# An fp32 first chunk, scores on row halves, and 512-column projections in a two-layer hybrid trunk

## The chip, the cores and the metric

The kernel runs on one core of a Trainium2 chip. The metric is the device time of one execution in microseconds (us). Before the change three runs took 942.56, 943.69 and 944.15 us, a median of 943.69 us. The profile below comes from one further execution.

TensorE (PE in the rows) multiplies matrices into PSUM; VectorE (DVE) and ScalarE (ACT) work on elements; GpSimd (POOL) does small masks and powers; SyncE (SP) issues nearly all DMAs.

## The reference

Two layers, each with a residual add, on 256 tokens of 1024 channels, all in float32:

```python
for layer in range(2):
    h = rmsnorm(x, norm_w)
    proj = h @ w_in          # 14368 columns: fq fk fv ff fg | sz sxbc sdt | dq dk dv dg | mg
    # A: softmax attention, 16 heads of 64, causal, scores shifted by cumulative log forget gates
    y_a = fox(fq, fk, fv, cumsum(log_sigmoid(ff))) * silu(fg)
    # B: causal depthwise conv (4 taps) + silu on x|B|C, chunked state-space scan, gated grouped norm
    y_b = rmsnorm_groups(ssd(silu(conv(sxbc)), softplus(sdt)) * silu(sz)) * ssm_norm_w
    # C: 8 heads of (softmax1 - lambda * softmax2) V, rotary on a quarter of q and k, per-head norm
    y_c = rmsnorm_heads(diff_attention(rope(dq), rope(dk), dv)) * silu(dg)
    gates = sigmoid(mg)      # three gates of 1024 channels
    merged = sum(gates[n] * (y[n] @ w_branch[n]) for n in (A, B, C))
    x = x + merged @ w_out
return rmsnorm(x, final_norm_w)
```

## The kernel before

**Projections.** All weights lie in HBM as *chunks* of at most 512 columns by 1024 rows, in the order in which they are used (`chunk_list`). A chunk is loaded in four *units* of 256 rows, 512 KB each, into a buffer `raw`. ScalarE rounds a unit to the one-pass format fp32r (`whi`, L231) and VectorE keeps what is left (`wlo`, L232). The activations are split the same way, and each product is the sum of three fp32r matmuls: hi by hi, hi by lo, lo by hi.

There are two forms. `bform` (L249) holds 128 tokens of the activation as the stationary operand and streams 512 weight columns: the result has tokens on partitions. `aform` (L264) holds 128 weight columns and streams all 256 tokens: the result has channels on partitions, as q, k, the conv inputs and the FoX gate need it. For one block of 128 columns and one of eight row blocks, `aform` issues three matmuls of 256 columns. One PSUM bank takes two column blocks, and the pool `pp` has three banks. There are 28 chunks in A form (14 in each layer) and 896 such triples.

**Around the projections.** `plan` lists the chunks of a layer as items. After each bank the loop calls `pump`, which lets waiting jobs (attention pairs, state-space groups, norms) emit a few instructions. A scheduler then orders each engine's instructions, so the order on an engine isn't that of the code.

**Scores.** q and k come out of `aform` with two heads on the two halves of the 128 partitions. `stack_q` and `stack_k` write, for each head, the hi and the lo part on top of each other (L380 to L388), so that two fp32r matmuls with 128 rows (L400, L401) give the head's scores. VectorE then adds the bias and takes the row maximum (L403), ScalarE takes the exponential (L406). For FoX the bias tile `sc` is loaded by two broadcast DMAs (L422, L423) from a scratch in HBM (`scr`, written at L371 from the cumulative gates that L359 to L366 compute), and GpSimd masks it twice (L426). There are 32 such head pairs in all, 16 in each layer: eight in FoX and eight in differential attention.

**The opening.** x is normalised, with the norm weight broadcast by DMA (L291, L210), transposed on TensorE (L198), split (L188, L189) and only then multiplied with the first chunk. TensorE transposes an identity 24 times first (L968).

**Buffers.** The pool `ap` has 41 pieces of 2 KB per partition; h's two halves take eight of them, the stacked q and k of four heads six. The PSUM pools `pp`, `pq`, `pt` have 3, 3 and 2 banks.

Of the kernel before, what the change touches and what calls it, by code (L numbers as in the profile page):

```python
# [34 lines left out]
WARM = 24  # L35
BEHIND = 1
ACTSQ = (2, 4)
# [12 lines left out]
def chunk_list():  # L50
    names = []
    names += [("fv0", [("w", FV, 512)]), ("fv1", [("w", FV + 512, 272)]),
              ("fv2", [("w", FV + 784, 240), ("w", FF, 16), ("w", SDT, 16)])]
# [6 lines left out]
             "mg10", "mg11", "wb10", "wb11", "mg20", "mg21", "wb20", "wb21", "wo0", "wo1"]  # L60
# [36 lines left out]
def trunk(ctx: ExitStack, tc: tile.TileContext, x, norm_w, weights, small, vectors,  # L97
# [13 lines left out]
    pq = ctx.enter_context(tc.tile_pool(name="pq", bufs=3, space=bass.MemoryType.PSUM))  # L111
    pt = ctx.enter_context(tc.tile_pool(name="pt", bufs=2, space=bass.MemoryType.PSUM))
# [9 lines left out]
    def halves():  # L122
        return tuple([a2(dtype=F32R) for _ in range(4)] for _ in range(2))

# [70 lines left out]
    def split_rows(src, hi, lo, tt, c):  # L195
        ps = bank(pt, "pt")
# [18 lines left out]
    def load_chunk(off, total, after=None, behind=()):  # L215
        units = []
        for u in range(UNITS):
            raw = wraw.tile([P, KU * 512], F32, name="raw")[:, 0:KU * total]
            o = off + u * KU * P * total
            ins = nc.sync.dma_start(raw, weights[o:o + KU * P * total].rearrange("(p f) -> p f", p=P)).ins  # L220
            if u == BEHIND:
                for late in behind:
                    tc.add_manual_dep(late, ins.name, mybir.DependencyInfo(
                        mybir.DependencyClass.NoSync, mybir.DependencyReason.DATA), reason="order")
            hi = wsp.tile([P, KU * 512], F32R, name="whi")[:, 0:KU * total]
            lo = wsp.tile([P, KU * 512], F32R, name="wlo")[:, 0:KU * total]
            with ExitStack() as es:
                if u > 0 and after:
                    for ins in after:
                        es.enter_context(tc.issue_after(ins))  # L230
                S.copy(out=hi, in_=raw)  # L231
                V.tensor_tensor(out=lo, in0=raw, in1=hi.bitcast(F32), op=ALU.subtract)  # L232
            units.append(tuple(t.rearrange("p (k n) -> p k n", k=KU) for t in (hi, lo)))
        return units, total

    ORDER = [(u, k, i) for u in range(UNITS) for k in range(KU) for i in range(3)]
    EARLY = [(u, k, i) for u, i in ((0, 0), (0, 1), (0, 2), (1, 0), (1, 2), (1, 1),
                                    (2, 0), (2, 2), (2, 1), (3, 0), (3, 2), (3, 1)) for k in range(KU)]
# [14 lines left out]
    def aform(ch, act, jj):  # L253
        units, n = ch
        ahi, alo = act
        ps = bank(pp, "pp")
        for u in range(UNITS):
            whi, wlo = units[u]
            for k in range(KU):
                kt = u * KU + k  # L260
                for j in range(2):
                    c0 = (2 * jj + j) * P
                    for i, (w, a) in enumerate(((whi, ahi), (whi, alo), (wlo, ahi))):
                        PE.matmul(ps[:, j * T:(j + 1) * T], lhsT=w[:, k, c0:c0 + P], rhs=at(a, kt),  # L264
                                  start=(kt == 0 and j == 0 and i == 0), stop=(kt == KT - 1 and j == 1 and i == 2))
        return ps

# [3 lines left out]
    def make_h(l, tt, xt, xs, ss, gap):  # L271
        st = L[l]
        if tt == 0:
            st["hT"] = halves()
# [54 lines left out]
    def small_chain(l, ps_by_tt):  # L329
# [26 lines left out]
        yield 2, 1.5  # L356
# [19 lines left out]
    LOH, HIH = slice(0, 64), slice(64, P)  # L376

    def stack_q(src, dst):
        for q, main, rest in zip(dst, (LOH, HIH), (HIH, LOH)):
            S.copy(out=q[main], in_=src[main])  # L380
            V.tensor_tensor(out=q[rest], in0=src[main], in1=q[main].bitcast(F32), op=ALU.subtract)

    def stack_k(src, dst):
        for k, kl, main, rest in zip(dst[0:2], dst[2:4], (LOH, HIH), (HIH, LOH)):
            S.copy(out=k[main], in_=src[main])
            V.tensor_tensor(out=kl[main], in0=src[main], in1=k[main].bitcast(F32), op=ALU.subtract)
            S.copy(out=k[rest], in_=src[main])
            S.copy(out=kl[rest], in_=kl[main].bitcast(F32))  # L388

    def split_qk(key, src):  # L390
        tiles = [a2(dtype=F32R) for _ in range(2 if key[1] == "q" else 4)]
        (stack_q if key[1] == "q" else stack_k)(src, tiles)
        return tiles

    def scores(st, pre, b, i, sc, bias, nm, rs):
        j, tk = b % 2, st[f"{pre}k{b // 2}"]
        q, k, kl = st[f"{pre}q{b // 2}"][i], tk[i], tk[2 + i]
        ps = bank(pq, "pq")
        for o, qs, n in ((0, slice(0, P), P), (P, slice(P, T), T)):
            PE.matmul(ps[:, o:o + n], lhsT=q[:, j, qs], rhs=k[:, j, 0:n], start=True, stop=False)  # L400
            PE.matmul(ps[:, o:o + n], lhsT=q[:, j, qs], rhs=kl[:, j, 0:n], start=False, stop=True)  # L401
        for t, sl in SPANS:
            V.tensor_tensor_reduce(out=sc[:, sl], in0=ps[:, sl], in1=bias[:, sl], scale=-0.125, scalar=BIG,  # L403
                                   op0=ALU.add, op1=ALU.min, accum_out=nm[:, t:t + 1])
        for t, sl in SPANS:
            S.activation(out=sc[:, sl], in_=sc[:, sl], func=AF.Exp, scale=-1.0,  # L406
                         bias=nm[:, t:t + 1], accum_out=rs[:, t:t + 1])
# [8 lines left out]
    def fox_pair(l, b, yhi, ylo):  # L416
# [7 lines left out]
        for i in (0, 2):  # L424
            v = sc[:, :, i * P:(i + 1) * P]
            G.affine_select(out=v, in_=v, pattern=[[0, 2], [-1, P]], compare_op=ALU.is_ge,  # L426
                            fill=NEG, base=0, channel_multiplier=1)
# [4 lines left out]
        for i in range(2):  # L432
            scores(st, "f", b, i, sc[:, i, :], sc[:, i, :], nm[:, i, :], rs[:, i, :])
# [58 lines left out]
    def ssd_cb(l):  # L492
# [16 lines left out]
        ps = bank(pt, "pt")  # L509
# [9 lines left out]
    def ssd_x(l, c, tt):  # L519
# [10 lines left out]
        ps = bank(pt, "pt")  # L530
# [12 lines left out]
    def ssd_group(l, g):  # L543
# [36 lines left out]
        ps = bank(pt, "pt")  # L580
# [67 lines left out]
    def rope(l, c):  # L648
# [19 lines left out]
        yield 1, 2.4  # L668
        for key, src in (("dq", q), ("dk", k)):
            for jj in range(2):  # L670
                st[f"{key}{2 * c + jj}"] = split_qk(key, src[jj])
            yield 1, 1.2 if key[1] == "k" else 2.4
# [6 lines left out]
    def diff_head(l, h):  # L679
        st, pr = L[l], par[l]  # L680
        yield from need(l, f"dq{h // 2}", f"dk{h // 2}")
        sc = sp.tile([P, 2, 384], F32, name="sc")
        nm = sm.tile([P, 2, 2], F32, name="dnm")
        rs = sm.tile([P, 2, 2], F32, name="drs")
        for i in range(2):
            scores(st, "d", h, i, sc[:, i, :], bmask, nm[:, i, :], rs[:, i, :])
# [40 lines left out]
    def plan(l):  # L727
# [39 lines left out]
        def t_evac(key):  # L767
            def f(jj, ps):
                st[f"{key[0:2]}{2 * int(key[2]) + jj}"] = split_qk(key, ps.rearrange("p (a t) -> p a t", t=T))
            return f  # L770

        def r_evac(key):
            def f(jj, ps):
                t = a2()
                st.setdefault("_" + key, []).append(t)
                S.copy(out=t, in_=ps.rearrange("p (a t) -> p a t", t=T))
                if jj == 1 and key[:2] == "dk":
                    start_job(rope, l, int(key[2]))
            return f

        def g_evac(key):
            def f(jj, ps):
                t = a2()
                p3 = ps.rearrange("p (a t) -> p a t", t=T)
                S.activation(out=t, in_=p3, func=AF.Tanh, scale=0.5)
                V.scalar_tensor_tensor(out=t, in0=t, scalar=1.0, in1=p3, op0=ALU.add, op1=ALU.mult)
                st[f"{key[0:2]}{2 * int(key[2]) + jj}"] = t
            return f

        def c_evac(key, j0):  # L790
# [11 lines left out]
            return f  # L802
# [90 lines left out]
        B("fv0", [v_evac("fv", 0, 512, False), v_evac("fv", 512, 272, False)])  # L893
        B("fv2", [v_evac("fv", 784, 240, True, fv_small)])
# [31 lines left out]
        mgroup(1)  # L926
        wgroup(1, "yB")
        mgroup(2)
# [12 lines left out]
        B("wb20", [wb_evac(2, 0), wb_evac(2, 1)], act=lambda: st["yC"], pre=load_res, wait="yC")  # L941
        B("wo0", [wo_evac(0), wo_evac(1)], act=lambda: st["mT"], flag="mT")
# [9 lines left out]
    def prefetch(n, after=None, behind=()):  # L952
        while queue and n > 0:
            l_, k_, _, off, m = queue.pop(0)
            loaded.append((l_, k_, load_chunk(off, m, after, behind)))
# [3 lines left out]
    xt = [rows() for _ in range(2)]  # L959

    def load_x(tt):
        for c in range(2):
            cs = slice(512 * c, 512 * c + 512)
# [101 lines left out]
```

## Time and profile before

| | |
|---|---|
| median of three runs | 943.69 us |
| profiled execution, its own time | 944.5 us |
| its span on the core | 942.8 us |
| PE busy | 928.9 us (99%) |
| DVE busy | 702.5 us (75%) |
| ACT busy | 596.7 us (63%) |
| DMA | 172.49 MB, mean 183 GB/s |

The profiled execution's own time is 1.7 us above its span. Busy time of PE counts a matmul to its modelled end, and consecutive matmuls overlap, so what a matmul costs is read from the distance between the starts of neighbours, not from its duration. A matmul of float32 operands that aren't fp32r shows as two records.

### The profile page before, as it was taken

Reading aid. Unit: us, or ns where it says so; the run is one execution under the profiler, and the core shown is the slowest. Engines: PE = TensorE matmul, PEld = TensorE weight load, DVE = VectorE, ACT = ScalarE, POOL = GpSimd, SP = SyncE. Lnnn points to the kernel's source line nnn. Section 1 sums busy time; section 2 is a strip of 40 time slices with the busy share of each in tenths; the row PEclk is TensorE's granted clock in tenths of the full one; section 3 lists DMA queues with packets and bytes.
Section 4 is the critical chain, followed back from the end, with each engine's and each line's share of the span. In section 5 each row is a group of like instructions: output and inputs, shape, how many; then the busy total and the mean of one; then the engine's idle time right before and its main releaser. Section 6 shows DMA issues by size and latency. Waiting matters only on the chain.

```text
span 942.8 us, 16557 instructions
## 1 busy us (share of the span) xinstructions
PE 928.9 (99%) x6076; PEld 831.4 (88%) x6076; DVE 702.5 (75%) x1440; ACT 596.7 (63%) x1131; POOL 37.2 (4%) x71
## 2 busy tenths in 40 slices
PE   6999999999999999999999999999999999999997
PEld 5999999988898988888889999998889999888886
DVE  5778788988666877864768778789877677787474
ACT  4668786655557868654546869666545596885441
POOL 1001100000000000100000110000000000010000
PEclk8999999999999999999999999999999999999999
DMA  7866735674555555555558664456646455554551
GB/s 223 278 208 205 218 112 158 188 242 148 176 188 177 181 185 171 167 163 197 190 176 279 195 222 137 140 179 201 203 155 197 158 186 190 190 171 155 181 184 45
DMA packets 60321, 172.49 MB, mean 183 GB/s; under 512 B 7312, under 2 KB 15824, under 8 KB 60240
## 3 DMA queue, kind: packets, MB, share of 16 engines
q1 hardware_dynamic: 59952, 170.91, 56.2%
q8 instruction: 48, 0.79, 0.3%
q10 hardware_dynamic: 288, 0.52, 0.1%
q14 instruction: 33, 0.27, 0.1%
HBM read 167.14 MB, written 2.16 MB: 180 GB/s over the span
## 4 chain that ended last, share of the span: by engine, by line
PE 90%; issue 7%; DMA 1%; DVE 0%; POOL 0%; ACT 0%; POOLq 0%; SPq 0%; DVEq 0%
PE pp L249 49%; PE pp L264 30%; PE pq L400 2%; PE pt L457 1%; PE pq L401 1%; PE pq L447 1%; PE pq L590 1%; PE pt L637 1%; PE pt L198 1%; PE pq L702 1%; PE pq L600 0%; PE pt L532 0%; DMA sc<-scr 0%; DMA scr<-sc_cum 0%; PE pt L709 0%
## 5 line engine op out<-in xcount | busy, mean ns | idle before, releaser
L249 PE MATMUL pp<-whi,a 128*128 128x512 f32 (+2 forms) x1488 | 451.3, 383 | 2.5 <-ACT a L188 1.6
L232 DVE TENSOR_TENSOR wlo<-raw,whi 128x1024 fp32r<-128x1024 f32 (+1 forms) x296 | 349.9, 1194 | 80.3 <-ACT whi L231 77.0
L231 ACT CAST whi<-raw 128x1024 fp32r<-128x1024 f32 (+1 forms) x296 | 302.1, 1028 | 119.3 <-PE pp L249 67.7
L264 PE MATMUL pp<-a,whi 128*128 128x256 f32 x1792 | 332.4, 285 | 0.0
L249 PEld LDWEIGHTS pp<-whi,a 128*128 128x128 f32 x1488 | 273.9, 188 | 55.8 <-ACT a L188 2.2
L264 PEld LDWEIGHTS pp<-a,whi 128*128 128x128 f32 x1792 | 281.2, 191 | 1.3 <-issue 1.0
L249 PE MATMUL pp<-wlo,a 128*128 128x512 f32 (+2 forms) x744 | 282.0, 381 | 0.1
L264 PE MATMUL pp<-a,wlo 128*128 128x256 f32 x896 | 254.4, 284 | 0.0
L264 PEld LDWEIGHTS pp<-a,wlo 128*128 128x128 f32 x896 | 171.5, 191 | 0.8 <-issue 0.8
L249 PEld LDWEIGHTS pp<-wlo,a 128*128 128x128 f32 x744 | 139.7, 188 | 25.8 <-DVE wlo L232 1.0
L477 DVE SCALAR_TENSOR_TENSOR a<-sw,pT,a 128x255 f32<-128x255 f32 (+2 forms) x96 | 42.0, 477 | 6.1 <-ACT a L474 6.0
L183 POOL TENSOR_TENSOR rstd<-rstd,mhalf 128x2 f32<-128x2 f32 (+2 forms) x24 | 17.8, 740 | 663.0 <-DVE rstd L181 642.1
L406 ACT ACTIVATE sc<-sc,dnm 128x128 f32<-128x128 f32 x64 | 28.6, 449 | 8.4 <-DVE dnm L403 8.3
L400 PE MATMUL pq<-a,a 128*128 128x128 f32 (+1 forms) x128 | 32.0, 285 | 0.5 <-DVE nm L403 0.5
L819 DVE SCALAR_TENSOR_TENSOR a<-a,pp 128x512 f32<-128x512 f32 x24 | 16.4, 683 | 20.6 <-PE pp L249 20.6
L188 ACT CAST a<-pt 128x256 fp32r<-128x256 f32 x32 | 11.4, 370 | 32.0 <-PE pt L198 25.8
L401 PE MATMUL pq<-a,a 128*128 128x128 f32 (+1 forms) x128 | 31.5, 269 | 0.0
L406 ACT ACTIVATE sc<-sc,nm 128x128 f32<-128x128 f32 (+1 forms) x64 | 28.4, 446 | 3.0 <-DVE nm L403 2.8
L403 DVE CUSTOM_DVE_ANT_0 sc<-pq,sc 128x128 f32<-128x128 f32 (+1 forms) x64 | 19.5, 351 | 7.4 <-POOL sc L426 6.6
L400 PEld LDWEIGHTS pq<-a,a 128*128 128x128 f32 x128 | 23.7, 190 | 1.3 <-DVE nm L403 0.9
L401 PEld LDWEIGHTS pq<-a,a 128*128 128x128 f32 x128 | 23.6, 191 | 0.3
L191 ACT ACTIVATE a<-pt,pT 128x256 fp32r<-128x256 f32 x32 | 14.8, 472 | 14.2 <-PE pt L637 12.4
(168 smaller groups left out, 811.8 us busy)
## 6 DMA issues: line engine op xcount, KB each, us to landing
raw<-in_weights_dram SPq DMA_DIRECT2D x280, 512.0 KB, 4.4
raw<-in_weights_dram SPq DMA_DIRECT2D x16, 272.0 KB, 3.4
sc<-scr SPq DMA_DIRECT2D x16, 256.0 KB, 5.6
a<-scr SPq DMA_DIRECT2D x16, 256.0 KB, 5.8
a<-in_x_dram SPq DMA_DIRECT2D x8, 256.0 KB, 5.4
sc<-scr SPq DMA_DIRECT2D x16, 128.0 KB, 5.2
a<-in_norm_w_dram SPq DMA_DIRECT2D x4, 256.0 KB, 7.0
rp<-a SPq DMA_DIRECT2D x32, 32.0 KB, 3.8
```

The source lines that it names most:

```text
L183: G.tensor_tensor(out=r[:, 0:width], in0=r[:, 0:width], in1=mhalf[:, 0:width], op=ALU.pow)
L191: S.activation(out=hi, in_=ps, func=AF.Copy, scale=scale)
L231: S.copy(out=hi, in_=raw)
L232: V.tensor_tensor(out=lo, in0=raw, in1=hi.bitcast(F32), op=ALU.subtract)
L249: PE.matmul(ps[:, 0:(c1 or n) - c0], lhsT=at(a, kt)[:, ts], rhs=w[:, k, c0:c1 or n], start=((u, k, i) == order[0]), stop=((u, k, i) == ord ...
L264: PE.matmul(ps[:, j * T:(j + 1) * T], lhsT=w[:, k, c0:c0 + P], rhs=at(a, kt), start=(kt == 0 and j == 0 and i == 0), stop=(kt == KT - 1 an ...
L400: PE.matmul(ps[:, o:o + n], lhsT=q[:, j, qs], rhs=k[:, j, 0:n], start=True, stop=False)
L401: PE.matmul(ps[:, o:o + n], lhsT=q[:, j, qs], rhs=kl[:, j, 0:n], start=False, stop=True)
L403: V.tensor_tensor_reduce(out=sc[:, sl], in0=ps[:, sl], in1=bias[:, sl], scale=-0.125, scalar=BIG, op0=ALU.add, op1=ALU.min, accum_out=nm[: ...
L406: S.activation(out=sc[:, sl], in_=sc[:, sl], func=AF.Exp, scale=-1.0, bias=nm[:, t:t + 1], accum_out=rs[:, t:t + 1])
L477: V.scalar_tensor_tensor(out=xc[:, s:T], in0=u[:, 0:T - s], scalar=pr["conv"](j, k), in1=xc[:, s:T], op0=ALU.mult, op1=ALU.add)
L819: V.scalar_tensor_tensor(out=t, in0=t, scalar=1.0, in1=ps, op0=ALU.add, op1=ALU.mult)
```

## The change

- `aform` takes one column block at a time. It streams h's hi and lo halves, which now lie side by side in one tile `both` (pool `hp`, one buffer), as 512 columns past `whi` (after: L269) and adds 256 columns of `wlo` by h's hi (L270). The two halves of the bank are then folded: ScalarE copies the right half, VectorE adds the left (L284, L285).
- q and k stay float32. The scores of two heads are float32 matmuls on 64 rows each, on the two row halves of the array and into two banks (L404). The first waits for an instruction on GpSimd, `held`: the last mask of `sc` in FoX, a small memset in differential attention.
- The opening computes the first chunk for the first 128 tokens with eight float32 matmuls on the unsplit weights (L1016). The norm weight is applied to the transposed x as a scale per partition, so that the broadcast isn't needed before; the order on four engines is written out.
- Pools: `ap` 41 to 26 pieces, `pq` 3 to 4 banks, `pt` 2 to 1; transposes move from `pt` to `pq`. `both` also takes branch C's output, so the items `mg2` (its last readers of h) go ahead of `wb1`, and the residual is loaded one item later.

```diff
-WARM = 24
+WARM = 16
+FILL = 6
...
-    ap = ctx.enter_context(tc.tile_pool(name="ap", bufs=41))
+    ap = ctx.enter_context(tc.tile_pool(name="ap", bufs=26))
...
+    def side_by_side():
+        both = hp.tile([P, KT, 2, T], F32R, name="both")
+        return both, tuple([both[:, 2 * i:2 * i + 2, s, :] for i in range(4)] for s in range(2))
...
+    def aform(ch, both, j):
         units, n = ch
         ps = bank(pp, "pp")
         for u in range(UNITS):
             whi, wlo = units[u]
             for k in range(KU):
+                kt, cols = u * KU + k, slice(j * P, (j + 1) * P)
+                PE.matmul(ps, lhsT=whi[:, k, cols], rhs=both[:, kt], start=(kt == 0), stop=False)
+                PE.matmul(ps[:, 0:T], lhsT=wlo[:, k, cols], rhs=both[:, kt, 0, :],
+                          start=False, stop=(kt == KT - 1))
...
+    def folded(f, new):
+        pair = []
+        def g(j, ps):
+            if j % 2 == 0:
+                pair.append(new())
+            d = pair[-1][:, j % 2, :]
+            S.copy(out=d, in_=ps[:, T:2 * T])
+            V.tensor_tensor(out=d, in0=ps[:, 0:T], in1=d, op=ALU.add)
+            if j % 2:
+                f(j // 2, pair[-1])
...
+    def scores(st, pre, b, sc, bias, nm, rs, held):
+        j, q, k = b % 2, st[f"{pre}q{b // 2}"], st[f"{pre}k{b // 2}"]
+        ps = [bank(pq, "pq") for _ in range(2)]
         for o, qs, n in ((0, slice(0, P), P), (P, slice(P, T), T)):
+            for i in range(2):
+                r = slice(64 * i, 64 * i + 64)
+                mm = PE.matmul(ps[i][:, o:o + n], lhsT=q[r, j, qs], rhs=k[r, j, 0:n], start=True, stop=True)
+                if o + i == 0:
+                    tc.add_manual_dep(mm.ins, held.name, ...)
...
+        def full(kt):
+            PE.matmul(first, lhsT=hf[kt // 4][:, kt % 4 * P:(kt % 4 + 1) * P],
+                      rhs=per_k(raw[kt // KU])[:, kt % KU, :], start=(kt == 0), stop=(kt == KT - 1))
...
+            for kt in range(6):
+                full(kt)
+            w_lo(0)
+            w_hi(1)
...
+            full(6)
+            p0 = turn(1, 0)
...
         mgroup(1)
+        mgroup(2)
         wgroup(1, "yB")
-        mgroup(2)
```

**The order on PE at the start.** These are the first rows before: identity transposes, the transposes of x (tiles a_142, a_143) and the first chunk's split products (a_149 to a_152 hold the hi half of h, a_153 to a_156 the lo half).

```order
L968 MATMUL pq<-ident 128x128 x24
L198 MATMUL pt<-ident,a_142 128x128 x4
L198 MATMUL pt<-ident,a_143 128x128 x4
L249 MATMUL pp<-whi,a_149 128x512 x2
L249 MATMUL pp<-wlo,a_149 128x512 x2
L249 MATMUL pp<-whi,a_153 128x512 x2
```

And these are the first rows now; wrow is the norm weight as 8 rows, a_112 to a_115 are the normalised rows of x, a_118 and a_119 the transposed first half of h, unsplit.

```order
L976 MATMUL pq<-ident 128x128 x16
L1038 MATMUL pq<-ident,wrow 128x8
L976 MATMUL pq<-ident 128x128 x6
L997 MATMUL pq<-ident,a_112 128x128 x4
L997 MATMUL pq<-ident,a_113 128x128 x4
L1016 MATMUL pp<-raw,a_118 128x512 x4
L1016 MATMUL pp<-raw,a_119 128x512 x3
L997 MATMUL pq<-ident,a_114 128x128 x4
L1016 MATMUL pp<-raw,a_119 128x512
L997 MATMUL pq<-ident,a_115 128x128 x4
L258 MATMUL pp<-whi,both 128x512 x4
```

Eight float32 matmuls on `raw` stand where 24 split ones stood, and the second half's transposes lie between them.

**The order on PE before the first FoX scores of the first layer.** Now the cumulative gates (L381 to L388) are followed by 22 pairs of L269 and L270, of which the first two and the last stand in these two pieces, and then by two head pairs of scores (a_720 is k, a_532 is q).

```order
L381 MATMUL pq<-sc_l,upper 128x16 x2
L386 MATMUL pq<-upper,sc_l 32x128
L387 MATMUL pq<-upper,sc_l 32x128
L388 MATMUL pq<-ones,sc_l 16x128
L270 MATMUL pp<-both,wlo 128x256
L269 MATMUL pp<-both,whi 128x512
```

```order
L269 MATMUL pp<-both,whi 128x512
L270 MATMUL pp<-both,wlo 128x256
L404 MATMUL pq<-a_720,a_532 128x128 x2
L404 MATMUL pq<-a_720,a_532 128x256 x2
L404 MATMUL pq<-a_720,a_532 128x128 x2
L404 MATMUL pq<-a_720,a_532 128x256 x2
```

In the second layer 35 such pairs stand there instead of 22. Before, the first scores stood after 19 matmuls of 256 columns and didn't wait for the bias.

**The order on SP at the same place.** Before, a weight unit stood between the scratch write and the broadcasts of the bias:

```order
L220 DMA raw<-in_weights_dram 128x1024 x17
L371 DMA scr_688<-sc_cum 32x256
L220 DMA raw<-in_weights_dram 128x1024
L422 DMA sc<-scr_688 128x2x128
L423 DMA sc<-scr_688 128x2x256
```

Now it doesn't:

```order
L222 DMA raw<-in_weights_dram 128x1024 x16
L393 DMA scr_605<-sc_cum 32x256
L429 DMA sc<-scr_605 128x2x128
L430 DMA sc<-scr_605 128x2x256
L429 DMA sc<-scr_605 128x2x128
```

Ahead of the scratch write 16 full units stand where 17 stood, and the eighteenth has moved behind the broadcasts.

## Rows read from the trace of the kernel before

**Rows 1.** The page: busy time, share, instructions; and granted clock by slice.

```profile
PE 928.9 (99%) x6076; PEld 831.4 (88%) x6076; DVE 702.5 (75%) x1440; ACT 596.7 (63%) x1131; POOL 37.2 (4%) x71
PEclk8999999999999999999999999999999999999999
```

**Rows 2.** The page: chain that ended last, shares by line.

```profile
PE pp L249 49%; PE pp L264 30%; PE pq L400 2%; PE pt L457 1%; PE pq L401 1%; PE pq L447 1%; PE pq L590 1%; PE pt L637 1%; PE pt L198 1%; PE pq L702 1%; PE pq L600 0%; PE pt L532 0%; DMA sc<-scr 0%; DMA scr<-sc_cum 0%; PE pt L709 0%
```

**Rows 3.** Groups by line and form: count, busy us, mean ns, idle before.

```profile
L264 PE MATMUL pp<-a,wlo 128*128 128x256 f32 x896 | 254.4, 284 | 0.0
```

**Rows 4.** Timeline of PE, an A-form stretch: start us, us, what, count.

```profile
41.18 0.40 PE L264 MATMUL pp<-a,whi 128*128 128x256 f32 x2
...
50.89 0.40 PE L264 MATMUL pp<-a,whi 128*128 128x256 f32 x2
```

**Rows 5.** Timeline of PE, a B-form stretch.

```profile
406.62 0.63 PE L249 MATMUL pp<-whi,a 128*128 128x512 f32 x2
...
410.03 0.40 PE L249 MATMUL pp<-whi,a 128*128 128x512 f32 x1
```

**Rows 6.** Timeline of PE, the scores of one pair of heads.

```profile
66.21 0.34 PE L400 MATMUL pq<-a,a 128*128 128x128 f32 x2
...
67.13 0.28 PE L264 MATMUL pp<-a,wlo 128*128 128x256 f32 x1
```

**Rows 7.** Timeline of PE, float32 matmuls on two column halves.

```profile
132.34 0.36 PE L264 MATMUL pp<-a,wlo 128*128 128x256 f32 x1
132.63 0.87 PE L457 MATMUL pt<-pT,a 128*64 128x256 f32 x8
133.43 0.88 PE L447 MATMUL pq<-ident,sc 128*128 128x128 f32 x6
```

**Rows 8.** Timeline of PE, float32 matmuls on the whole array.

```profile
375.43 0.38 PE L708 MATMUL pt<-a,pT 128*128 128x128 f32 x2
375.65 0.39 PE L709 MATMUL pt<-a,pT 128*128 128x128 f32 x2
```

**Rows 9.** Timeline of PE, the opening.

```profile
2.03 4.35 PE L968 MATMUL pq<-ident 128*128 128x128 f32 x24 [2.03 <-POOL mhalf L147]
8.68 1.08 PE L198 MATMUL pt<-ident,a 128*128 128x128 f32 x4 [2.30 <-DVE a L210]
...
11.90 1.22 PE L249 MATMUL pp<-whi,a 128*128 128x512 f32 x2 [0.71 <-ACT a L188]
...
22.36 0.50 PE L249 MATMUL pp<-whi,a 128*128 128x512 f32 x1 [0.85 <-ACT a L188]
...
40.47 0.40 PE L264 MATMUL pp<-a,whi 128*128 128x256 f32 x2
```

**Rows 10.** Timelines of POOL and ACT, the opening.

```profile
5.54 0.55 POOL L183 TENSOR_TENSOR rstd<-rstd,mhalf 128x1 f32<-128x1 f32 x1 [3.10 <-DVE rstd L181]
...
10.53 1.04 ACT L231 CAST whi<-raw 128x1024 fp32r<-128x1024 f32 x1 [6.19 <-DMA raw<-in_weights_dram]
```

**Rows 11.** Busy time by stretch, the opening: PE, PEld, DVE, ACT, POOL, clock, DMA.

```profile
9.00:12.00 3.00, 1.98 (x9) 1.18 (x7) 1.14 (x2) 1.32 (x2) 0.00 (x0) 0.50 1.03 413
...
16.00:18.00 2.00, 1.92 (x8) 1.27 (x8) 2.00 (x2) 2.00 (x8) 0.00 (x0) 1.00 0.32 115
```

**Rows 12.** Timelines of PE, SP and POOL, the first layer's first FoX scores.

```profile
60.67 0.38 PE L366 MATMUL pq<-ones,sc_l 128*16 128x128 f32 x2
...
64.54 0.35 SPq L220 DMA_DIRECT2D raw<-in_weights_dram  x1
...
71.56 0.81 POOL L426 TENSOR_SCALAR_AFFINE_SELECT sc<-sc 128x256 f32<-128x256 f32 x2 [0.33 <-DMA sc<-scr]
```

**Rows 13.** Groups on DVE: weight splits (the page), adds and splits from PSUM.

```profile
L232 DVE TENSOR_TENSOR wlo<-raw,whi 128x1024 fp32r<-128x1024 f32 (+1 forms) x296 | 349.9, 1194 | 80.3 <-ACT whi L231 77.0
...
L597 DVE TENSOR_TENSOR a<-a,pq 128x256 f32<-128x256 f32 x16 | 5.9, 412 | 0.0
L386 DVE TENSOR_TENSOR a<-pp,a 64x512 fp32r<-64x512 f32 x16 | 11.0, 688 | 6.6 <-ACT a L385 6.1
```

More of the change, by code (lines that the diff above doesn't have):

```diff
@@ L213, in trunk, with load_raw, split_hi @@
     chunks, _ = chunk_list()
-    def load_chunk(off, total, after=None, behind=()):
+    def load_raw(off, total, u):
+        raw = wraw.tile([P, KU * 512], F32, name="raw")[:, 0:KU * total]
+        o = off + u * KU * P * total
+        nc.sync.dma_start(raw, weights[o:o + KU * P * total].rearrange("(p f) -> p f", p=P))
+        return raw
+    def split_hi(raw, total):
+        hi = wsp.tile([P, KU * 512], F32R, name="whi")[:, 0:KU * total]
+        S.copy(out=hi, in_=raw)
+        return hi
@@ L221, in load_chunk @@
[L221 to L232, printed above, removed]
@@ L259, in aform, with wide @@
             for k in range(KU):
[L260 to L265, printed above, removed]
-        return ps
+                kt, cols = u * KU + k, slice(j * P, (j + 1) * P)
+                PE.matmul(ps, lhsT=whi[:, k, cols], rhs=both[:, kt], start=(kt == 0), stop=False)
+                PE.matmul(ps[:, 0:T], lhsT=wlo[:, k, cols], rhs=both[:, kt, 0, :],
+                          start=False, stop=(kt == KT - 1))
+        return ps
+    def wide():
+        return tp.tile([P, 2, T], F32, name="sw")
+    def folded(f, new):
[8 more added lines that the diff above has]
+                f(j // 2, pair[-1])
+        return g
     scr_x = dr.tile([2, P, D], F32, name="scr_x")
@@ L273, in make_h @@
         if tt == 0:
-            st["hT"] = halves()
+            st["both"], st["hT"] = side_by_side()
         with tc.high_priority(URGENT):
@@ L374, in trunk @@
     SPANS = ((0, slice(0, P)), (1, slice(P, 384)))
[L376 to L388, printed above, removed]
@@ L431, in fox_pair @@
         rs = sm.tile([P, 2, 2], F32, name="rs")
-        for i in range(2):
-            scores(st, "f", b, i, sc[:, i, :], sc[:, i, :], nm[:, i, :], rs[:, i, :])
+        scores(st, "f", b, sc, lambda i: sc[:, i, :], nm, rs, held)
         ri = sm.tile([P, 2, 2], F32, name="ri")
@@ L682, in diff_head @@
         sc = sp.tile([P, 2, 384], F32, name="sc")
+        held = G.memset(sc[:, 0, 0:1], 0.0).ins
         nm = sm.tile([P, 2, 2], F32, name="dnm")
         rs = sm.tile([P, 2, 2], F32, name="drs")
-        for i in range(2):
-            scores(st, "d", h, i, sc[:, i, :], bmask, nm[:, i, :], rs[:, i, :])
+        scores(st, "d", h, sc, lambda i: bmask, nm, rs, held)
         ri = sm.tile([P, 2, 2], F32, name="dri")
@@ L950, in trunk, with prefetch @@
     loaded = []
-    def prefetch(n, after=None, behind=()):
+    def prefetch(n):
         while queue and n > 0:
             l_, k_, _, off, m = queue.pop(0)
-            loaded.append((l_, k_, load_chunk(off, m, after, behind)))
+            loaded.append((l_, k_, load_chunk(off, m)))
             n -= 1
     constants()
[L959 to L963, printed above, removed]
-            yield nc.sync.dma_start(xt[tt][c], x[0, tt * P:(tt + 1) * P, cs]).ins
```

265 lines of the change are left out of this document (164 added, 101 removed).

## The prediction

> **What bounds the kernel now.** I read the page first. PE is busy 99% of the span and the granted clock is full after the first slice [rows 1]; 79% of the chain that ended last are the two projection lines on PE [rows 2]. DVE and ACT have room on the mean. So after the opening a change is worth what it does to the sum of PE's start-to-start distances, plus new waits on PE. The groups by form give the counts, and the timeline the distances.
>
> An A-form matmul of 256 columns costs 119.9 ns: 81 starts lie between 41.18 and 50.89 us [rows 4]. A B-form matmul of 512 columns costs 227 ns: 15 starts in 3.41 us [rows 5]. Twice the columns cost 107 ns more, so some 13 ns of each matmul are not columns. A pair of heads' scores costs 0.92 us (66.21 to 67.13) [rows 6].
>
> **The change part by part.**
>
> *A form.* Three times 896 matmuls of 256 columns [rows 3] become 896 of 512 and 896 of 256. The columns are the same; 896 fixed costs go. A triple costs 3 x 119.9 = 359.7 ns now, the new pair 227.3 + 119.9 = 347.2. 896 x 12.5 = **-11.2 us**, all on the path. Both prices are in rows and only their mixture is not: ends 0 (the short matmul after a long one costs what the rest of the triple did) and -12.
>
> By the Trainium skill (TensorE: Matmul & The Clock Gate, section Back-to-back issue gap) a warm matmul has a fixed cost of about 2.5 ns beside its columns. By that this term would be some -2.2 us; the rows show five times as much per matmul, and the rows decide.
>
> *Scores.* 32 pairs. Four float32 matmuls stand in place of eight fp32r ones. A whole-array float32 matmul of 128 columns takes 0.22 us, in two records [rows 8], so 4 x its columns. If the row halves run beside each other, a pair is 128 + 256 columns, four times: 0.64 us. No row shows row halves. The nearest is the FoX output on two column halves, with exactly this mix (two matmuls of 256 columns, two of 128, eight records) [rows 7]: its neighbour starts at 132.34, it at 132.63 and the next at 133.43. Less the neighbour's own 0.12 us, the group takes 0.97. So the halves overlap (in a row they would take 1.28), and 0.33 us go at the two ends, where the array changes its partition. I take 0.97, and 0.05 more because 128 stationary columns are loaded where these had 64: +0.10 x 32 = 3.2. Eight pairs stand right behind another pair and save the ends between them, some 0.27: -2.1. In each layer one pair stands with its halves one after the other: 2 x 0.64 = 1.3. Sum **+2.4 us**. Ends: 0.64 with nothing at the ends, -9; the halves in a row with the loss, 1.55, +20.
>
> The Trainium skill (TensorEngine Tiling (Array Packing), section Tiling Modes) says that changing the tiling mode, as opposed to the tile, drains TensorE. The ends of that FoX group agree: 0.33 us beside 0.64. It speaks against this part: without drains the term would be -9.
>
> *Opening.* PE's first real product starts at 11.90 us, the second half of the tokens at 22.36, and from there PE runs without a gap into the first A-form chunk at 40.47 [rows 9]. The start waits for the norm broadcasts and for the first weight unit behind them, which lands at 10.53, while the reciprocal root was there at 6.09 [rows 10]. From 9 to 12 us the clock is at half speed, 1.2 GHz, after PE had stood from 6.38 to 8.68; from 16 us it is full [rows 9, 11]. Now the broadcasts are issued behind two weight units and x's second half; I put the first unit at 6.5 us, x scaled at 7.2, transposed and copied at 8.6. The eight float32 products take 4 x 0.222 = 0.89 us each, 7.1 in all (24 split ones would take 5.4, so this costs 1.7): 15.7. The second half's 8 transposes add 0.9, its split before the next matmul 0.85 as now [rows 9], the last weight unit and the `wlo` units that VectorE makes late some 1.2. The second half so starts at 18.7 instead of 22.36: **-3.7 us**. Ends: -6 without waits; +1 if the clock stays at half for as long as now and VectorE, which still has to split this chunk and the next, is late for both.
>
> *The wait for `held`.* Before, the first scores run at 66 us, and VectorE waits for the bias; now PE waits, with all projections behind it in its queue. In the first layer the gates' last matmuls start at 60.67, and the second mask for the first pair, the first of the two in this row, ends at 71.97 [rows 12]: 11.3 us later. Now PE has 22 pairs of 347 ns between: 7.6 us. The weight unit at 64.54, ahead of the first broadcast [rows 12], is no longer there; a transfer of 512 KB less in front should give back 1.5 to 2 us. The wait is 3.7 if nothing is saved and 1.7 if 2 us are; I take **+2.0 us**, ends 0 and +4. In the second layer 35 pairs, 12.1 us, cover the same path: nothing. The memset that stands for the mask in differential attention needs only a free buffer: nothing.
>
> *Evacuation.* VectorE loses 64 splits of 0.69 us and gains 112 adds of 0.41 [rows 13]; ScalarE gets 112 half-bank copies in place of more and longer casts. On the mean this costs nothing, with PE as cover. But a bank of `pp` now holds 8 x 347 = 2.8 us of work where it held 5.8, so with three banks the copy and the add have 5.6 us before PE waits, where they had 11.5. Four unit splits in a row are 4.8 us of VectorE (1.194 each [rows 13]). No row shows such a wait. I put **+1.5 us** for this, one bank of `pt`, and 26 pieces; ends 0 and +10. Pieces are not scarcer than they were: `both` takes eight off and q and k 16.
>
> *Moved items.* `mg2` before `wb1` adds no instruction; branch C's split waits for `mg2` behind the cover of `wb1` (96 x 227 ns = 21.8 us). The six loads of the residual and the norm weight now stand behind the last branch weights, 21.8 us of `wb2` ahead of their use: nothing; without that cover PE would wait for 1.5 MB.
>
> Sum: -11.2 + 2.4 - 3.7 + 2.0 + 1.5 = **-9.0 us**. The profiled execution took 944.5 us: 935.5. It lies 0.8 above the median of the runs, so I predict **934.7 us**.
>
> **Rivals.**
>
> 1. *The row halves don't overlap.* The two halves take two passes through the array one after the other: 1.55 us a pair against 0.92, from the first pair on. Instead of +2.4 the scores cost +20: 934.7 + 17.6 = 952, slower. For it: no row shows row halves, and a single pair in each layer is even laid out that way. Against: column halves overlap nearly fully [rows 7], and the two heads write different banks. Chance 0.10.
> 2. *The banks bind.* In the FoX and conv stretches the fold comes late, and PE waits for `pp` at the 28 chunks, 0.35 us each: +10 in place of +1.5, 943. It decides once copy and add lag their bank by over 5.6 us. For it: the slack is halved and the fold needs two engines in turn. Against: with 99% busy [rows 1] PE waits almost nowhere for a bank now. Chance 0.12.
> 3. *Nothing is lost.* The opening gains 6, `held` and the banks cost nothing, the scores come out even: -11.2 - 6 = -17, 926.5. Chance 0.10.
> 4. *The fixed cost stays.* The 512 + 256 pair costs the triple's 360 ns: 934.7 + 11.2 = 946, slower or the same. By the page's 2.5 ns named above it would be 943.7. Against it stand both prices in rows. Chance 0.04.
>
> **How the numbers follow.** The forecast has 0.64. A measurement of this kernel can tell about 0.2% (1.9 us) from no change. The forecast and rival 3 are faster nearly throughout (0.72 of 0.74), rival 2 in part (0.07 of 0.12, 0.04 the same), rival 4 the same or slower, rival 1 slower: faster 0.80, same 0.08, slower 0.12. The range takes in the forecast's own ends and most of rivals 2 and 3, and leaves out rival 1: 926.5 to 944.
>
> **What would show it.** A form: starts 227 and 120 ns apart in turn, some 311 us for the 1792 matmuls. Scores: a pair's eight records in some 0.97 to 1.05 us, its two heads' starts a few ns apart; serial halves would show as 1.3 and more. Opening: the first float32 product near 8.6 us and the first A-form matmul near 36.8. `held`: one idle stretch of PE of about 2 us with the mask as its releaser, in the first layer alone. Banks: idle PE in front of L269 released by DVE L285. It is wrong if the A-form pair costs 360 ns, or if PE's idle time behind the opening comes to more than 8 us.

## The result, and the profile after

The changed kernel took 958.66 us (median of five runs, 954.59 to 959.12) against 943.69: a ratio of 1.0152, 95% interval 1.0141 to 1.0163. It is slower by 1.5%; 934.7 us was predicted. The profiled execution took 958.99 us, its span is 957.2.

The page after, beside [rows 1]:

```profile
PE 930.9 (97%) x5171; PEld 773.8 (81%) x5171; DVE 698.6 (73%) x1497; ACT 538.6 (56%) x1083; POOL 43.0 (4%) x87
PEclk9989999999999999999999999999999999999999
```

905 PE instructions fewer, less work on ScalarE, and yet a longer span in which PE is busy 97% of the time instead of 99%. The waits of PE after (engine, line, releaser: us in total, times, longest) say where to look:

```profile
PE pp L269 <- DVE a L285: 6.0, 2, 5.1
PE pq L643 <- ACT a L770: 5.0, 2, 2.5
PE pq L404 <- POOL sc L433: 2.2, 2, 2.0
PE pq L404 <- DVE ri L441: 1.7, 2, 0.9
```

And in the stretches behind the three largest kinds the granted clock is half, 1.2 GHz (each row: length, busy us of PE, PEld, DVE, ACT and POOL, then the granted clock, the DMA's busy share and GB/s):

```profile
48.50:55.33 6.83, 5.81 (x18) 4.94 (x19) 5.49 (x13) 3.48 (x6) 0.00 (x0) 0.50 0.54 160
400.07:403.48 3.41, 3.41 (x12) 2.83 (x11) 0.78 (x3) 0.74 (x4) 0.70 (x1) 0.50 0.43 175
536.60:540.02 3.42, 3.42 (x13) 2.44 (x10) 3.26 (x21) 3.01 (x13) 1.05 (x3) 0.50 0.85 303
867.70:871.11 3.41, 3.41 (x12) 3.05 (x13) 0.23 (x2) 0.74 (x4) 0.50 (x1) 0.50 0.76 278
```

PE had stood for 5.13, 2.51, 1.98 and 2.51 us ahead of them; before, the clock stayed full behind the opening [rows 1, 11]. The starts of the same work in both traces give the place of each loss (us):

| PE starts | before | after | difference |
|---|---|---|---|
| first A-form matmul (`fq0`) | 40.47 | 35.75 | -4.7 |
| second A-form chunk (`fk0`) | 51.97 | 54.80 | +2.8 |
| behind the last A-form chunk of layer 1 | 329.37 | 331.73 | +2.4 |
| first A-form matmul of layer 2 | 500.71 | 507.05 | +6.3 |
| its fourth chunk (`fq1`) | 540.86 | 550.92 | +10.1 |
| behind the last A-form chunk of layer 2 | 789.82 | 800.03 | +10.2 |
| last matmul | 936.36 | 950.71 | +14.3 |

The opening's gain is lost within one chunk, and the rest goes in three short places. The same difference by kind, as sums of PE's start-to-start distances, with waits of over 0.15 us and the surplus of projections at half clock taken out and shown by themselves:

| us | before | after | e8 (below) |
|---|---|---|---|
| first A-form matmul starts | 40.47 | 35.75 | 36.4 |
| A-form matmuls | 326.0 | 320.2 | 319.7 |
| scores, with the ends they cost the neighbours | 29.6 | 28.8 | 28.6 |
| waits behind the opening | 0.5 | 16.6 | 6.4 |
| half clock behind the opening, projections | 0 | 6.5 | 0 |

Work and opening give back 11.3 us (4.7 + 5.8 + 0.8); waits and half clock take 22.6; 3.0 us more lie in small matmuls, 2.4 of them the differential heads beside their waits, in part at half clock: together the +14.3.

**The largest wait.** ScalarE, VectorE and PE after, around 44 us (idle before, and releaser, in brackets; rows between these are left out):

```profile
41.44 0.40 PE L270 MATMUL pp<-both,wlo 128*128 128x256 f32 x2
41.97 1.05 ACT L227 CAST whi<-raw 128x1024 fp32r<-128x1024 f32 x1 [1.74 <-DMA raw<-in_weights_dram]
44.11 0.28 PE L270 MATMUL pp<-both,wlo 128*128 128x256 f32 x1
44.23 1.04 ACT L227 CAST whi<-raw 128x1024 fp32r<-128x1024 f32 x1 [1.21 <-DMA raw<-in_weights_dram]
46.69 1.04 ACT L227 CAST whi<-raw 128x1024 fp32r<-128x1024 f32 x1 [1.41 <-DMA raw<-in_weights_dram]
47.64 0.91 ACT L284 COPY a<-pp 128x256 f32<-128x256 f32 x3
49.05 0.75 DVE L285 TENSOR_TENSOR a<-pp,a 128x256 f32<-128x256 f32 x2
49.52 0.80 PE L269 MATMUL pp<-both,whi 128*128 128x512 f32 x1 [5.13 <-DVE a L285]
```

By the semaphore events of the trace the first bank of `fq0` is full at 41.7 us (the first L270 of the first row ends it), the second at 42.2 and the third at 44.4. PE fills the first two by turns, as the last weight unit of `fq0` itself comes late (its cast starts at 37.91, its `wlo` split ends at 40.22). The first fold copy (L284) runs at 47.64, 5.9 us behind its bank, not because ScalarE is busy (it idles 1.2 to 1.7 us before each of these casts), but because it stands in ScalarE's queue behind the four casts of the *next* chunk, the last three of which are shown; their weights haven't landed. The first add ends at 49.46. Three banks are full, so PE waits.

**The wait before yC's transposes.** Around 396.5 us:

```profile
396.31 0.39 PE L716 MATMUL pt<-a,pT 128*128 128x128 f32 x2
396.73 0.28 ACT L720 ACTIVATE sc<-pt 128x128 f32<-128x128 f32 x1 [0.72 <-PE pt L716]
397.36 0.29 ACT L720 ACTIVATE sc<-pt 128x128 f32<-128x128 f32 x1
397.77 0.17 DVE L185 TENSOR_SCALAR rstd<-ss 128x2 f32<-128x2 f32 x1 [0.28 <-ACT sc L720]
398.08 0.70 POOL L187 TENSOR_TENSOR rstd<-rstd,mhalf 128x2 f32<-128x2 f32 x1 [5.61 <-DVE rstd L185]
398.81 0.61 DVE L723 SCALAR_TENSOR_TENSOR a<-pt,rstd,a 128x128 f32<-128x128 f32 x2 [0.87 <-POOL rstd L187]
399.31 0.30 PE L643 MATMUL pq<-ident,a 128*128 128x128 f32 x1 [2.51 <-ACT a L770]
```

The row of PE names a gate's evacuation (L770), which ended just before; but the instruction reads what L723 writes, and the chain from L716 over ScalarE, VectorE and GpSimd to L723 fills the whole gap. A transpose of yC stands right behind a head's output in PE's queue, with no projection between, and needs that head's norm.

### The profile page after: what moved, and what is told of

It is laid out like the page before. It is cut to its first block, busy times and chain, and to the rows that moved or that the text cites. A ratio compares the mean times of both kernels' runs of the same rounds, so it can differ in the third digit from the quotient of the medians.

```text
span 957.2 us, 14793 instructions
## 1 busy us (share of the span) xinstructions
PE 930.9 (97%) x5171; PEld 773.8 (81%) x5171; DVE 698.6 (73%) x1497; ACT 538.6 (56%) x1083; POOL 43.0 (4%) x87
## 4 chain that ended last, share of the span: by engine, by line
PE 77%; issue 8%; DVE 6%; DMA 4%; ACT 3%; POOL 1%; SPq 1%; POOLq 0%; ACTq 0%; DVEq 0%
PE pp L258 45%; PE pp L269 15%; PE pp L270 8%; DVE wlo L232 2%; PE pq L404 2%; DMA raw<-in_weights_dram 2%; PE pt L463 1%; PE pq L453 1%; ACT sc L413 1%; ACT whi L227 1%; PE pq L596 1%; PE pq L643 1%; DMA a<-scr 1%; DVE a L483 1%; SPq L673 1%
## 5 line engine op out<-in xcount | busy, mean ns | idle before, releaser
L269 PE MATMUL pp<-both,whi 128*128 128x512 f32 x896 | 324.5, 403 | 6.6 <-DVE a L285 6.0
L258 PE MATMUL pp<-whi,both 128*128 128x512 f32 (+1 forms) x1072 | 324.5, 382 | 0.6 <-ACT a L770 0.6
L270 PE MATMUL pp<-both,wlo 128*128 128x256 f32 x896 | 254.8, 285 | 0.0
L258 PEld LDWEIGHTS pp<-whi,both 128*128 128x128 f32 x1072 | 198.5, 189 | 38.7 <-ACT a L770 1.0
L269 PEld LDWEIGHTS pp<-both,whi 128*128 128x128 f32 x896 | 170.0, 190 | 50.0 <-DVE a L285 6.7
L258 PE MATMUL pp<-wlo,both 128*128 128x512 f32 (+1 forms) x536 | 202.7, 380 | 0.8 <-DVE wlo L232 0.8
L270 PEld LDWEIGHTS pp<-both,wlo 128*128 128x128 f32 x896 | 171.1, 191 | 3.3 <-issue 2.9
L258 PE MATMUL pp<-whi,a 128*128 128x512 f32 (+1 forms) x400 | 123.8, 387 | 0.5 <-DVE a L820 0.5
L258 PEld LDWEIGHTS pp<-whi,a 128*128 128x128 f32 x400 | 74.0, 188 | 15.5 <-DVE a L820 0.9
L284 ACT COPY a<-pp 128x256 f32<-128x256 f32 x64 | 23.1, 369 | 51.1 <-PE pp L270 51.1
L285 DVE TENSOR_TENSOR a<-pp,a 128x256 f32<-128x256 f32 x64 | 26.2, 419 | 33.1 <-ACT a L284 32.9
L258 PEld LDWEIGHTS pp<-wlo,a 128*128 128x128 f32 x200 | 37.7, 188 | 6.9
L413 ACT ACTIVATE sc<-sc,nm 128x128 f32<-128x128 f32 x64 | 28.5, 447 | 14.7 <-DVE nm L410 14.6
L404 PE MATMUL pq<-a,a 64*128 64x128 f32 (+1 forms) x256 | 28.1, 347 | 3.9 <-POOL sc L433 2.2
```

What stands on the lines that cost most here:

```text
L258: PE.matmul(ps[:, 0:(c1 or n) - c0], lhsT=at(a, kt)[:, ts], rhs=w[:, k, c0:c1 or n], start=((u, k, i) == order[0]), stop=((u, k, i) == ord ...
L269: PE.matmul(ps, lhsT=whi[:, k, cols], rhs=both[:, kt], start=(kt == 0), stop=False)
L270: PE.matmul(ps[:, 0:T], lhsT=wlo[:, k, cols], rhs=both[:, kt, 0, :], start=False, stop=(kt == KT - 1))
L284: S.copy(out=d, in_=ps[:, T:2 * T])
L285: V.tensor_tensor(out=d, in0=ps[:, 0:T], in1=d, op=ALU.add)
L404: mm = PE.matmul(ps[i][:, o:o + n], lhsT=q[r, j, qs], rhs=k[r, j, 0:n], start=True, stop=True)
```

## The experiments

All times are medians; the runs of before beside them had medians of 943.5 to 944.0, and each ratio is to these, with its 95% interval in brackets.

**e1: casts behind the folds.**

```diff
-            S.copy(out=d, in_=ps[:, T:2 * T])
+            copies.append(S.copy(out=d, in_=ps[:, T:2 * T]).ins)
...
-            prefetch(it["n"])
+            with ExitStack() as es:
+                if it["key"] == "fk0" and l == 0:
+                    es.enter_context(tc.issue_after(copies[1]))   # second fold copy of fq0
+                prefetch(it["n"])
```

> The changed kernel, in which ScalarE's four casts of the second A-form chunk (fk0) stand behind the first two fold copies of fq0 instead of ahead of them. Theory 'waits': the change's loss is PE's waits and the half clock behind them, and the largest (5.13 us at 44.1 us, with 6.83 us at half clock behind it) is there because the fold copies stand behind casts whose weights land late. Then it goes to under 1.5 us, no half-clock stretch follows, and the time falls by 5 to 8.5 us from 958.7: 950 to 954. Rival 'late weights': the weights of fk0 land when they land, so PE waits as long a few us later, for whi or wlo of fk0: 957 to 959.

950.82 us, ratio 1.0073 (1.0045 to 1.0102). ScalarE there:

```profile
42.55 0.85 ACT L286 COPY a<-pp 128x256 f32<-128x256 f32 x2 [2.59 <-PE pp L270]
43.29 3.89 ACT L227 CAST whi<-raw 128x1024 fp32r<-128x1024 f32 x4
```

The copies now wait for PE, whose first bank is full at 42.5, and four casts run back to back on landed weights. `fk0` starts at 49.2 instead of 54.8, and the A-form chunks of layer 1 end at 324.8 instead of 331.7; no wait of over 0.42 us stands from 25 to 110 us, and no half clock. The trace is of e1's shortest execution (947.07 us), so the gain is better read as 6.9 us over this stretch, or as 7.8 by the medians. That much of the loss was one queue order; late weights by themselves were not the cause.

**e2: no hold on the scores.**

```diff
-                if o + i == 0:
-                    tc.add_manual_dep(mm.ins, held.name, ...)
```

> The changed kernel without the dependency of a pair's first score matmul on the mask. Theory 'waits': the 1.98 us at 533.1 us in the second layer and the 3.41 us at half clock behind it go: 3 to 4 us less, 954.5 to 956. Rival 'banks': the scores run early and hold two of the four shared banks until VectorE has the mask, and the next user of a shared bank waits instead: within 1 us of 958.7.

972.31 us, ratio 1.0309 (1.0287 to 1.0331): 13.6 us worse. Both expectations are wrong. PE's waits:

```profile
PE pq L404 <- DVE a L285: 11.0, 5, 4.8
PE pp L269 <- DVE a L285: 5.8, 2, 4.9
```

Without the hold the scheduler puts a pair's scores right behind the chunk that makes their k, and PE waits for the fold of that k, which stands in VectorE's queue behind weight splits (ahead of the wait that ends at 80.19 us, two of them from 77.44 on, the fold at 79.71). The hold costs 2 us once and keeps 11 away.

**e3: two pt banks, three shared ones.**

```diff
-    pq = ctx.enter_context(tc.tile_pool(name="pq", bufs=4, ...))
-    pt = ctx.enter_context(tc.tile_pool(name="pt", bufs=1, ...))
+    pq = ctx.enter_context(tc.tile_pool(name="pq", bufs=3, ...))
+    pt = ctx.enter_context(tc.tile_pool(name="pt", bufs=2, ...))
```

> The changed kernel with three shared banks and two pt banks, as before. Theory 'one pt bank': the waits of 2.51 us at 396.5 and 864.9 us are the last differential heads taking turns on the single pt bank, so both go, with 3.41 us at half clock behind each: 6 to 9 us less, 950 to 953. Rival 'shared tile': they come from yC's place in the tile of h and from mg2 being moved, and stay: within 1.5 us of 958.7, or above it where three shared banks are too few for two heads' scores.

974.43 us, ratio 1.0325 (1.0303 to 1.0346). The 2.51 us waits are gone (no wait before yC's transposes in the trace), so the split into four banks and one is needed for them; but the time rises: 16 of the 32 pairs now run their two heads one after the other, in the trace. That the second head finds no free bank among three is argued from the pool's size; no row names it. The changed kernel, a pair of heads, and e3, one head (PE, eight and four records):

```profile
108.40 0.93 PE L404 MATMUL pq<-a,a 64*128 64x128 f32 x8
109.26 0.50 PE L269 MATMUL pp<-both,whi 128*128 128x512 f32 x1
```

```profile
80.70 0.92 PE L404 MATMUL pq<-a,a 64*128 64x128 f32 x4
81.55 0.51 PE L269 MATMUL pp<-both,whi 128*128 128x512 f32 x1
```

Two heads take 0.86 us from start to next start, one head alone 0.85. By sums the scores take 43.5 us in e3 against 28.8. The Trainium skill (TensorEngine Tiling (Array Packing), section Gotcha 1: PSUM Pressure) says that row tiles write to different banks and so press on PSUM; these runs agree: 14.7 us more with one bank less.

**e4: the old opening**, with the loads and the first chunk as before:

```diff
-    ch0, ps0, tail = opening()
+    list(load_x(0))
+    load_nwb(0)
+    x1 = list(load_x(1))
...
+        it["evac"][0](0, bform(ch, act, 0, EARLY))
```

> The changed kernel with the opening of before. Theory 'waits': the opening's 4.7 us are lost again because the weights of fk0 and the casts cannot come earlier, so the first A-form matmul starts near 40.5 instead of 35.75, but the 5.13 us wait and the half clock behind it nearly go: 954 to 957. Rival 'a real gain': the opening's gain reaches the end, the bank wait has nothing to do with it: 962 to 964.

952.20 us, ratio 1.0094 (1.0077 to 1.0111), less than either theory expected: the first A-form matmul starts at 40.1, and the wait at 44 us is gone, though a cast of the next chunk still stands ahead of the first fold:

```profile
43.25 1.05 ACT L236 CAST whi<-raw 128x1024 fp32r<-128x1024 f32 x1 [0.32 <-DMA raw<-in_weights_dram]
44.20 0.37 ACT L280 COPY a<-pp 128x256 f32<-128x256 f32 x1
```

PE is 4.3 us later here, the weights are nearly there, and the copy runs 1.1 us behind its bank (full at 43.05) instead of 5.9. The banks also fill one after the other (43.05, 45.88, 48.70), so PE has two more to fill meanwhile. The faster opening is what makes the queue order harmful.

**e5: before, with the new A form alone** (h in one tile, 33 pieces; q and k split from the folded tile):

```diff
-                    ev(s, aform(ch, it["act"](), s))
+                    for j in (2 * s, 2 * s + 1):
+                        ev(j, aform(ch, L[l]["both"], j))
```

> The kernel before with the new A form alone: h in the one tile, 512 + 256 columns, fold by ScalarE and VectorE; q and k are then split from the folded tile, which is one pass more than in the changed kernel. Theory 'waits': the A-form matmuls take 5.8 us less in sum (320.2 us against 326.0 in the two traces, PE's waits left out), and what is lost is waits for a pp bank, each named DVE's add as the releaser: 938 to 945. Rival 'the pair is dear': its matmuls themselves take as long as the triples, 326 us or more in sum, so 944 or more with no waits at all.

967.75 us, ratio 1.0243 (1.0213 to 1.0273). The matmuls took 320.4 us, so the pair is not dear; but waits behind the opening came to 17.7 us, 8.6 of them for VectorE's last step of the conv evacuation and 4.5 for its fold, with two stretches of 6.83 us at half clock. The expected size was wrong. That VectorE is late here because it has a fold *and* the splits of q and k is likely, but no run separates the two.

**e6: before, with the new scores and their banks alone** (and, with them, the change's chunk borders and the residual loaded one item later):

```diff
-        for i in range(2):
-            scores(st, "f", b, i, sc[:, i, :], sc[:, i, :], nm[:, i, :], rs[:, i, :])
+        scores(st, "f", b, sc, lambda i: sc[:, i, :], nm, rs, held)
```

> The kernel before with the row-half scores, their four shared banks and single pt bank, the mask wait, and the change's chunk borders; opening, A form, the place of yC and the order of mg2 as before. Theory 'waits': a pair costs about what it did (28.8 us against 29.6 in sum), and the waits come along: 0.9 us twice for the shared banks, 1 to 2 us for the mask in each layer, 2.5 us twice before yC if the single pt bank makes them: 945 to 952. Rival 'scores pay': fewer copies and splits leave ScalarE and VectorE early, no such waits: 938 to 942.

957.01 us, ratio 1.0137 (1.0122 to 1.0152), slower than the bounds. Scores 29.4 us against 29.6: no gain, no loss. The mask alone makes waits of 2.35, 3.16 and 0.55 us, with 6.83 us at half clock from 533.1 us on. In front of yC's transposes PE doesn't wait, with one `pt` bank and `mg2` in its old place.

**e7 and e8: e1 with mg2 behind wb1 again, and that with yC in its own pieces.**

```diff
-        mgroup(2)
         wgroup(1, "yB")
+        mgroup(2)
```

(and the same in the chunk order; e8 also `yhi, ylo = halves()` for yC and 33 pieces)

> The changed kernel with the casts of fk0 behind the folds (e1, 950.8) and mg2 behind wb1 again, as before; yC still takes h's tile. Theory 'order of mg2': the 2.5 us waits in front of yC's transposes and the half clock behind them go, and a wait of 1 to 1.5 us for yC's first split comes behind mg2 in each layer: 944 to 948. Rival 'one pt bank': the last heads still take turns on it, the 2.5 us waits stay: 950 to 952.

> As the run before (casts behind the folds, mg2 behind wb1), and yC in eight pieces of its own, with 33 pieces. Theory: without the shared tile no wait for yC's first split is left, 942 to 946. Rival 'one pt bank': 950 to 952 as without it.

e7: 943.56 us, ratio 0.9997 (0.9987 to 1.0006); e8: 941.72, ratio 0.9983 (0.9974 to 0.9993), the one version that beats both kernels. The 2.51 us waits and their half clock go with the order of mg2, although one `pt` bank stays: the wait needs both, the split into four banks and one and the order. Each median lies just under its bounds. e7 is 1.8 us slower than e8 (ten runs each, 941.5 to 945.4 and 940.7 to 944.0). By kind the waits are alike, 1.8 us for yC's split in e7 against 2.1 for a gate in e8, and in sum e7 has 0.9 us more behind the opening. So yC in h's tile, or the 26 pieces that go with it, may cost up to 1.8 us; no run separates these two. Of e8's waits:

```profile
PE pp L258 <- ACT a L772: 2.1, 2, 1.1
PE pq L406 <- DVE ri L443: 1.7, 2, 0.9
PE pq L406 <- POOL sc L435: 1.7, 2, 0.9
```

**e9 and e10: e8 with later scores; and spread** (the second edit in e10 alone):

```diff
-        yield 1, 0.0        # behind the mask
+        yield 2, 0.0
-        yield 2, 2.2        # behind the scores
+        yield 2, 3.0
```

> As e8 (941.7), with a FoX pair's scores one slot later, some 6 us of A-form matmuls more ahead of the first ones. Theory 'waits': the two waits for the mask in the second layer, 0.92 and 0.77 us, go, and nothing waits instead: 939 to 941. Rival 'later is late': the heads pile up, and the next users of the shared banks or the gate of branch A wait: 942 to 946.

> As e9, and a FoX pair's scores take the whole budget of a slot, so that no two pairs stand in one. Theory 'waits': the 0.87 us before the fourth pair in each layer, for a shared bank, go as well: 937.5 to 940. Rival: pairs apart from each other pay their ends each, 0.075 us by the trace of the changed kernel, and nothing else moves: 941 to 943.

943.24 and 943.23 us, ratios 0.9995 (0.9986 to 1.0004) and 0.9998 (0.9987 to 1.0009): no gain on e8. The 0.87 us for a shared bank go in both. The two waits for the mask that e9 aims at stay (0.93 and 0.78 us), and in e10 one of them does (0.93). Others come: 1.08 us for a conv fold in e9, 1.01 us twice before `ssd_x` in e10, which waits for VectorE.

**e11 and e12: e8 with the old opening (the edit of e4); with the old A form** (the edit of e5 turned round, the banks copied out as they were).

> As e8 with the opening of before (the order of casts and folds is then left to the scheduler, as in e4). Theory 'the opening is worth its 4 us once the casts stand right': 944 to 947. Rival 'its gain is lost to late weights whatever the order': 941 to 943.

> As e8 with the A form of before (triples of 256 columns, no fold, two column tiles to a bank). Theory: the A form's matmuls are worth 5.8 us by the sums of the traces and its fold brings 1 to 2 us of waits, so without it 945 to 948. Rival 'the fold costs what the columns save': 940 to 943.

944.28 us, ratio 1.0006 (0.9997 to 1.0014): the opening is worth 2.6 us of its 4, once the queue is right. 950.80 us, ratio 1.0065 (1.0048 to 1.0082), above the expected 945 to 948: without the new A form 9.1 us more, 7.0 of them in the matmuls (326.7 against 319.7). The waits behind the opening have the same sum (6.2 against 6.4 us), but one of them is 3.04 us for the mask, and behind it PE runs 6.83 us at half clock, which takes some 3 us (an estimate from the distances of starts there); the A form starts 1.0 us earlier.

## Why the prediction was wrong, step by step

The prediction named its own sign of being wrong, over 8 us of idle PE behind the opening: it was 16.6. Part by part:

- *A form*, -11.2: **-5.8**. Right in sign, half in size. The medians are 233 and 117 ns, 350 a pair (347.2 predicted, 359.7 the triple). Three starts of one stretch:

```profile
37.38 0.39 PE L269 MATMUL pp<-both,whi 128*128 128x512 f32 x1
37.61 0.28 PE L270 MATMUL pp<-both,wlo 128*128 128x256 f32 x1
37.73 0.39 PE L269 MATMUL pp<-both,whi 128*128 128x512 f32 x1
```

  An undisturbed bank takes 2.77 us in some places and 2.83 in others, where 24 matmuls at the old price [rows 4] took 2.88; why two values, no run tells. By the medians the pair saves 8.7 us; short pauses under 0.15 us take the rest. The fixed cost of about 2.5 ns a matmul that the Trainium skill (TensorE: Matmul & The Clock Gate, section Back-to-back issue gap) states doesn't fit either: 350 ns are 30 above the columns of the two (768 at 2.4 GHz).
- *Scores*, +2.4: **-0.8**. The halves overlap as the column halves did [rows 7], and a pair is cheaper than that row let expect: 0.86 us. Rival 1 did not come; e3 shows its effect, heads one after the other, where one bank is missing.
- *Opening*, -3.7: **-4.7** at the first A-form matmul (35.75; 36.8 predicted; the first float32 product at 8.80, predicted 8.6). The step was right up to that point and not followed beyond it: with the old opening (e4) the four casts ahead of the folds delay the first copy by 1.1 us, with the new one by 5.9.
- *Evacuation*, +1.5, **is the step that failed first**. It set a slack of 5.6 us against copy and add, which last 0.37 and 0.42 us. Both sides were wrong. The lag is set by the queue, not by the duration: copy and add were done 7.7 us behind the full bank (41.7 to 49.5), because casts waiting for DMA stood ahead of them. And the slack was 2.7 us (41.7 to 44.4), as PE had filled the first two banks by turns. Rival 2 had the mechanism and its point (5.6 us of lag), but spread it over 28 chunks; it was one place, 5.13 us and the half clock behind it. e1 gives 7.8 back by the medians.
- *`held`*, +2.0 in the first layer alone: it was 0.19 there and **1.98 in the second**, priced at nothing. In the first layer the step failed by its count: the trace has 32 pairs between the gates and the first scores (58.2 to 69.9 us), not the 22 given ahead of the prediction, and they cover the path, 10.3 us (57.9 to 68.2), which is 1.0 us shorter than before, where 1.5 to 2 were expected. (The first scores of before ran at 63.4, not 66 us.) In the second PE covers 12.8 us (520.4 to 533.2), no less than the 12.1 counted, but the path took 14.9:

```profile
519.66 3.83 SPq L222 DMA_DIRECT2D raw<-in_weights_dram  x4
524.35 0.33 SPq L393 DMA_DIRECT2D scr<-sc_cum  x1
528.96 0.39 SPq L429 DMA_DIRECT2D sc<-scr  x1
532.68 4.15 POOL L433 TENSOR_SCALAR_AFFINE_SELECT sc<-sc 128x256 f32<-128x256 f32 x6 [45.06 <-DMA sc<-scr]
535.35 0.49 PE L404 MATMUL pq<-a,a 64*128 64x128 f32 x4 [1.98 <-POOL sc L433]
```

  The small write L393 is followed by its reader 4.6 us later, with four weight units issued just ahead of it; it lands at 528.90, just behind the last of them (528.74). In the first layer it was 2.0 us (60.42 to 62.38). VectorE had the cumulative gates ready 3.9 us after PE's last gate matmul instead of 2.5, and the two masks of the pair took 2.6 us instead of 2.3 in the first layer and 0.8 before [rows 12] (last section).
- *Moved items*, "nothing": **5.0 us of waits** and two half-clock stretches, from `mg2` ahead of `wb1` together with one `pt` bank. yC in h's tile, which the step looked at, costs some 1.8 us at most (e7 against e8).
- *The clock* was in no term. Each of these waits was counted, if at all, by its own length; behind four of them PE ran at 1.2 GHz for 3.4 to 6.8 us, which cost 6.5 us more in the projections.

The page said that PE waits almost nowhere [rows 1]; that held for the old order of the queues. The prediction took over the cover and changed the lengths, but not the order in which a scheduler would put casts, folds and transposes, although the order of the built kernel was there to be read. With the queue orders put right (e8) the change is worth some 2 us, not 9: the A form gives 6.3 us, the opening 4.1 and the scores 1.0, but 5.9 us of new waits stay, and the rest goes in small matmuls.

## What to carry to other kernels

An evacuation's slack is not bank time less its own duration: read what stands ahead of it in its engine's queue, above all casts that wait for DMA. When one stage gets faster, look for the queue order that its old length had hidden. Reckon with a stretch at half clock behind a long PE wait, as behind the waits of 1.98 to 5.13 us here, though not behind every one. And expect row-tiled matmuls that are one shared bank short to lose their overlap, here in 16 of 32 pairs.

## What the runs showed of the hardware that was not expected

- Half clock came behind PE waits of 1.98, 2.51 and 5.13 us, and not behind those of 0.87 us in the same trace. No case is sure: in e1 the clock stayed full behind a wait of 2.51 us at 389.9 us and was half behind its twin at 853.4; in e6 it stayed full behind 2.35 us; in e4 two waits of 0.91 and 0.78 us, 1.7 us apart, had half clock behind them (532.3 us), and in e8 the same two (0.92 and 0.77) had not.
- GpSimd's mask (one line, 32 times; ns as least, median, most):

```profile
L433 POOL TENSOR_SCALAR_AFFINE_SELECT sc<-sc x32: 403/409/1389, 66.0 to 573.6; 128x256 f32<-128x256 f32 x32
```

  It takes 0.40 to 0.42 us alone and 1.0 to 1.4 where a weight split of VectorE (two inputs from SBUF) runs beside most of it; the slowest of these splits take 1.42 to 1.43 us where the median is 1.22. The Trainium skill (GPSIMD Engine Reference, section 1. Specifications) says that GpSimd shares its SBUF interfaces with VectorE, with contention from instructions of two SBUF inputs; the trace agrees.
- A float32 score on half the rows costs the same alone as with its neighbour on the other half, 0.85 against 0.86 us, and the second half's record starts 6 ns behind the first.
